# A transformer block in float32: fewer, larger transfers for each attention head, and softmax statistics through DRAM

## The chip, the cores and the metric

The kernel runs on one core of one Trainium2 chip. The metric is device microseconds of one execution; lower is better. A core has TensorE (PE, with its weight loads shown apart as PEld), VectorE (DVE), ScalarE (ACT), GpSimd (POOL) and SyncE (SP). SP does no arithmetic here: it issues nearly all DMA transfers, in the order of its own instruction stream, and sixteen DMA engines carry them out.

## The reference

One block of a model: normalization, one wide projection, a gated causal convolution of 31 taps, dilated attention of 16 heads, gates, an output projection, and a feed-forward part with a convolution of 3 taps. Sequence 1024, width 1024, head width 64, all in float32. What matters here is the attention:

```python
for window, dilation in ((128, 1), (512, 4), (2048, 16)):
    o_g, lse_g = dilated_window_attention(q, k, v, slopes, window, dilation)
    outs.append(o_g); lses.append(lse_g)
mix = jax.nn.softmax(jnp.stack(lses), axis=0)
o = jnp.einsum('gbsh,gbshd->bshd', mix, jnp.stack(outs))
y_b = o @ w_attn_out[l]
```

Each query sees keys at distances up to 128, every fourth up to 512, and every sixteenth up to 2048. Mixing three softmaxes by their log sums is the same as one softmax over all these keys, with a key counted once for each group that reaches it; the kernel computes that, with the counts and the distance slopes folded into a mask that is prepared on the host.

## The kernel before

Every float32 matrix product is made of rounded parts: an operand is split into a high part and a low part (`split`, L84), and the products high by high, high by low and low by high are summed. For the attention scores the two parts of the queries are interleaved on the 128 partitions (partition 2d holds the high part of channel d, 2d+1 the low part), so that one product with the high part of the keys, doubled onto both partitions, and one with the low part give the sum (`scored`, L922).

The stages, in order of time: normalization and the gated inputs; queries, keys and values (to about 410 us), whose parts go to DRAM scratch, `dq` and `dk` (L157, L158, written by `spill` in `qkv_tail`, L634) and `dv`; gates by a Strassen-like scheme while DVE runs the convolution; the attention (about 570 to 872 us); the output projections; the feed-forward part.

The attention loop (L1106 on) runs over slots `at`: 16 heads, two halves of the tokens, four steps each, so eight slots, called places 0 to 7, to a head. In places 0 to 3 the first 512 queries are scored against near keys. In place 4 come the far rows: for each of the four residues r modulo 4, queries of the second half against keys of the first half at multiples of 4 (`("far",)`). In places 5 to 7 the second half's near keys follow (blocks 7, 6, then 4 and 5). For each tile DVE adds the mask and takes the least value (`least`, L926), ACT makes the powers and their sum (`powers`, L964). The products with the values come twelve slots later (`BACK = 12`): the tiles are transposed on PE (`flip`, L1007), split by ACT and DVE into `ph` and `pl`, and multiplied by the values (`weigh`, L1041); `result` (L1057) copies the sum from PSUM and sends it to DRAM scratch `do_`. PE also has other work laid between by `fill`: gate and convolution-output products.

The second half of a head has near and far tiles with separate maxima and sums. Before the tiles are scaled, the two kinds must be brought together, and they lie in different orders: near statistics have one partition for each query of a block of 128, far statistics have one partition for each query of a residue class. `own` (L976) is a tile of 128 x 2 x 4 x 2 numbers: near or far, block or residue, least value or sum. `other` holds the counterparts in the other's order. `far_to_near` (L984) and `near_to_far` (L980) each move 4 KB in four transfers between them, `far_to_near` two slots after the far tile's slot, `near_to_far` one slot after the last near tile's. `compare` (L988) on DVE reads both nine slots after the far tile's slot, `combine` (L994) one slot later; then POOL scales the tiles (`times`, L967).

`head(h)` (L740) loads the next head's operands in place 1: for each part s of the queries, `q[s:P:2]`; for each partition parity s, the keys' high part to `kh[s:P:2]` and low part to `kl[s:P:2]`; and the mask. That is seven transfers. `values` (L905) loads the values in place 5 with two more. Each tile has two buffers. POOL makes reordered copies of a part of q, kh and kl for the far rows (`by_residue`, L918).

After the loop has issued its last scores, the outputs come back: `o_fetch` (L1073) loads the two parts of `do_` (products with the values' high and low part) for two channel blocks at a time, `o_step` (L1080) adds and splits them, and the product with the output weights `w_ao` follows. `w_ao` is laid out on the host (`_layout`).

Order: inside the attention loop ACT, DVE, PE and POOL follow the text (L1102). SP does not: its transfers are ordered by the framework's planner, which simulates the program and issues what is ready, earlier text first. A transfer that reads what another wrote, in DRAM too, waits on SP for that transfer to land.

Of the kernel before, what the change touches and what calls it, by code (L numbers as in the profile page):

```python
# [13 lines left out]
F32 = mybir.dt.float32  # L14
F32R = mybir.dt.float32r
# [6 lines left out]
P = 128  # L22
D = 1024
T = 1024
KT = D // P
H = 16
DH = 64
# [8 lines left out]
FRONT = (1, 1, 0, 0, 0, 0, 1, 0)  # L36
BEHIND = (1, 0, 1, 0, 2, 1, 1, 1)
BACK = 12
COPIES = (-1, 0, 1)
APART = (2, 3, 4, 5, 6)  # L40
START = (1, 1, 1, 1, 0, 0, 0, 0, 0, 0, 0, 0)
# [19 lines left out]
def block_kernel(ctx: ExitStack, tc: tile.TileContext, x, xT, x0, g2, pack, mask,  # L61
# [88 lines left out]
    def spill(dst, src):  # L150
        sp.dma_start(dst.bitcast(F32), src.bitcast(F32))

    def fetch(dst, src):
        sp.dma_start(dst.bitcast(F32), src.bitcast(F32))


    dq = [[dr.tile([P, 4, T], F32R, name=f"dq{i}_{a}") for a in range(2)] for i in range(2)]  # L157
    dk = [[dr.tile([P, 4, T], F32R, name=f"dk{i}_{a}") for a in range(2)] for i in range(2)]  # L158
    dv = [dr.tile([T, 8, P], F32R, name=f"dv{i}") for i in range(2)]
    dh = dr.tile([P, KT, T], F32, name="dh")  # L160
    db12 = [dr.tile([P, 4, 512], F32R, name=f"db12_{i}") for i in range(2)]
    dgate = [dr.tile([P, T], F32, name=f"dgate{i}") for i in range(16)]
    da = dr.tile([P, KT, T], F32, name="da")
    dya = [dr.tile([P, T], F32, name=f"dya{i}") for i in range(8)]
    do_ = [dr.tile([P, KT, T], F32, name=f"do{i}") for i in range(2)]
    dff = [dr.tile([P, T], F32, name=f"dff{i}") for i in range(FT)]
    dx2 = [dr.tile([P, D], F32, name=f"dx2_{i}") for i in range(8)]
    dform = [[dr.tile([P, 1024], F32R, name=f"dform{f}_{i}") for i in range(7)] for f in range(3)]

    HALVES = (slice(0, 512), slice(512, 1024))  # L170
# [134 lines left out]
    if True:  # L305
# [313 lines left out]
        def qkv_tail(ch, tt, qn):  # L619
            kind, g8 = ch % 3, ch // 3  # L620
            pt = big_ps(f"qt_{ch}_{tt}")[:, 0:512]
            for j in range(4):
                pe.transpose(pt[:, j * P : (j + 1) * P], qn[:, j * P : (j + 1) * P], ident)
            qh = p1a.tile([P, 512], F32R, tag="qh", bufs=2, name=f"qh_{ch}_{tt}")
            ql = p1a.tile([P, 512], F32R, tag="ql", bufs=2, name=f"ql_{ch}_{tt}")
            if kind == 0:
                act.activation(qh, pt, AF.Copy, scale=qkg)
                dve.scalar_tensor_tensor(out=ql, in0=pt, scalar=qkg, in1=qh.bitcast(F32),
                                         op0=ALU.mult, op1=ALU.subtract)
            else:  # L630
                split(qh, ql, pt)
            dst = dq if kind == 0 else dk
            for s, t in ((0, qh), (1, ql)):
                spill(dst[g8][s][:, :, tt * P : (tt + 1) * P], t.rearrange("p (a b) -> p a b", a=4))  # L634

        tails = []
        for ch in range(6):
# [102 lines left out]
        def head(h):  # L740
            hp, r, g8 = h // 2, (h % 2) * DH, h // 8
            q = p2.tile([P, T], F32R, tag="q", bufs=2, name=f"q_{h}")
            kh = p2.tile([P, T], F32R, tag="kh", bufs=2, name=f"kh_{h}")
            kl = p2.tile([P, T], F32R, tag="kl", bufs=2, name=f"kl_{h}")
            m = p2.tile([P, 640], F32, tag="m", bufs=2, name=f"m_{h}")
            for s in range(2):
                fetch(q[s:P:2, :], dq[g8][s][r : r + DH, hp % 4, :])
                fetch(kh[s:P:2, :], dk[g8][0][r : r + DH, hp % 4, :])
                fetch(kl[s:P:2, :], dk[g8][1][r : r + DH, hp % 4, :])
            sp.dma_start(m, mask[h])  # L750
            return q, kh, kl, m

        cover(COVER)
        firsts = [gate_weights(a)[1] for a, _ in PAIRS[:2]]
# [142 lines left out]
    if True:  # L897
# [82 lines left out]
        def near_to_far(h):  # L980
            for i in range(4):
                sp.dma_start(other[h][32 * i : 32 * i + 32, 1], own[h][:, 0, i])

        def far_to_near(h):  # L984
            for i in range(4):
                sp.dma_start(other[h][:, 0, i], own[h][32 * i : 32 * i + 32, 1])

        def compare(h):  # L988
            f = ready2("both", [P, 2, 4], F32, 2, f"both_{h}")
# [65 lines left out]
            return (h, half) if last else None  # L1055

        def result(h, half):  # L1057
            r = (h % 2) * DH
            o = outs.pop((h, half))
            cs = slice(half * 512, half * 512 + 512)  # L1060
            tmp = ready2("ot", [P, 512], F32, 2, f"ot_{h}_{half}")
            read_out[h, half] = act.activation(tmp.rearrange("p (i a r) -> p i a r", i=4, r=4),
                                               o.rearrange("p (i r a) -> p i a r", i=4, r=4), AF.Copy)
            for i in range(2):
                sp.dma_start(do_[i][r : r + DH, h // 2, cs], tmp[i * DH : (i + 1) * DH, :])

        def fill(n):
            for _ in range(n):
# [3 lines left out]

        def o_fetch(half, k):  # L1073
            cs = slice(half * 512, half * 512 + 512)
            raw = stage(do_[0][:, k : k + 2, cs], f"o_{half}{k}").rearrange("p (a b) -> p a b", a=2)
            hi, lo = (oT[i][half][:, k : k + 2, :] for i in range(2))
            fetch(lo, do_[1][:, k : k + 2, cs])
            return raw, hi, lo

        def o_step(new):  # L1080
# [21 lines left out]
        with tc.manual_schedule(engines={ENG.Activation, ENG.DVE, ENG.PE, ENG.Pool}):  # L1102
            apart = lambda at: at % 8 in APART or not 0 <= at < len(slots)
            pend = []
            fill(1)
            for at in range(len(slots) + BACK + 1):  # L1106
                count[2] += 1
                cur = slots[at] if at < len(slots) else None
                front, behind = (FRONT[at % 8], BEHIND[at % 8] + (START[at] if at < BACK else 0)) if cur else TAIL
                new = []  # L1110
                if cur is not None:
                    h, half, n = cur
                    place = at % 8
                    if place == 4:
                        statistics(h)
                    if place == 5:
                        values(h)
                    if place == 1 and h + 1 < H:
                        tiles[h + 1] = head(h + 1)
                    new = score(h, tiles[h], SCORES[half][n])  # L1120
                for unit in late:
                    share(*unit)
                if len(pieces) > 2 and apart(at):
                    piece_high(2)
                fill(front)
                for n, soon in enumerate(COPIES):
                    if at == 0 and soon < 0 or cur is not None and (at - soon) % 8 == 0 and at - soon < len(slots):
                        by_residue((at - soon) // 8 if at else 0, n)
                flips = []
                if BACK <= at < len(slots) + BACK:  # L1130
                    fh, fhalf, fn = slots[at - BACK]
                    if FLIPS[fhalf][fn]:
                        flips.append(flip(fh, fhalf, FLIPS[fhalf][fn]))
                for w in pend:
                    done = weigh(*w) or done
                pend = flips
                late = []
                if done is not None:
                    result(*done)
                    done = None  # L1140
                for ago, ready in ((BACK - 2, combine), (BACK - 3, compare)):
                    if 0 <= at - ago < len(slots) and slots[at - ago][1:] == (1, 0):
                        ready(slots[at - ago][0])
                for unit in new:
                    powers(*unit)
                if cur is not None and half == 0:
                    late = new
                for ago, n0, send in ((2, 0, far_to_near), (1, 3, near_to_far)):
                    if 0 <= at - ago < len(slots) and slots[at - ago][1:] == (1, n0):
                        send(slots[at - ago][0])  # L1150
                if at == len(slots):
                    p2_cm.__exit__(None, None, None)
                    hb2.append(ctx.enter_context(tc.tile_pool(name="hb2a", bufs=1, reuse_waits="tile")))
                    oT = [[hb2[0].tile([P, KT, 512], F32R, tag=f"hb{a}0", name=f"oT{a}0")] for a in range(2)]
                    heads = [o_fetch(0, k) for k in range(0, KT - 2, 2)]
                if at - len(slots) in (4, 5, 8, 9, 10, 11, 12):
                    o_step(heads)
                if at == len(slots) + BACK - 4:
                    heads.append(o_fetch(0, KT - 2))
                if apart(at):  # L1160
                    piece_low()
                fill(behind)
                if apart(at + 1):
                    piece_high(2)
            for _ in gates:
                piece_low()
                piece_high()
                o_step(heads)
# [579 lines left out]
def _layout(a):  # L1748
# [24 lines left out]
        "w_ch": w_ch,  # L1773
        "w_qkv": row(w_in[:, 2048:5120], 6),
        "w_co": col(a["w_conv_out"][0], 8),
        "w_ao": col(a["w_attn_out"][0], 8),
        "w_o": row(a["w_out"][0], 2),
        "w_up": col(a["w_up"][0], 2 * FT),
        "w_down": np.ascontiguousarray(a["w_down"][0].reshape(FT, P, D)),
# [13 lines left out]
```

## Time and profile before

| | |
|---|---|
| time, median of 3 runs | 1700.63 us (1699.92 to 1704.21) |
| profiled execution, its own time | 1702.94 us |
| its span, first to last instruction | 1701.1 us |
| mean granted TensorE clock | 0.998 |
| PE busy | 1685.4 us (99% of the span) |
| DVE, ACT, POOL busy | 1288.9, 786.0, 222.6 us |
| DMA: moved, mean rate | 300.21 MB, 176 GB/s |
| transfers of the statistics in all (`other<-own`) | 128, of 1 KB each |

The profile is one execution. A line of instructions gives its start, its duration, the engine, the line of the kernel, the operation with output and input tile, and, in square brackets, how long the engine had been idle before it and what ended that idle time. A line of waits gives the total in us, how many times, and the longest. On SP the duration of a transfer's line is that of the issue alone; the time from issue to landing is given apart.

### The profile page before, as it was taken

To read this page: it belongs to the slowest core of one execution; us is meant where nothing else is said; L and a number is where in the kernel's file an instruction comes from. 1 tells how busy PE (TensorE), PEld (TensorE's weight loads), DVE (VectorE), ACT (ScalarE), POOL (GpSimd) and SP (SyncE) were. 2 spreads that over 40 slices of the span, in tenths; PEclk is the share of its full clock that TensorE was granted. 3 is DMA by queue.
4 is the path that set the end of the run, shared out by engine and by line. 5 is a ranking of instruction groups with operands and counts; after the bars stand their busy time and mean duration, and the time that the engine had idled before them with its cause. 6 is when DMAs were issued, how large, how long until landed. Compare 5 with 4: busy or idle time off the path is not lost.

```text
span 1701.1 us, 22933 instructions
## 1 busy us (share of the span) xinstructions
PE 1685.4 (99%) x8003; PEld 1406.2 (83%) x8003; DVE 1288.9 (76%) x2098; ACT 786.0 (46%) x1351; POOL 222.6 (13%) x300
## 2 busy tenths in 40 slices
PE   9999999999999999999999999999999999999999
PEld 7888888888888888888878888888888888888887
DVE  5999999999876467756657654887777777889863
ACT  5411233233245477767745433554554455543431
POOL 0000132033000245445410000000000000000000
PEclk9999999999999999999999999999999999999999
DMA  9411145344555977777769694622222222498851
GB/s 373 152 50 50 50 136 161 124 136 137 186 170 196 312 218 240 246 226 232 209 191 340 202 337 143 235 87 87 75 87 87 86 76 80 153 382 302 289 167 50
DMA packets 186867, 300.21 MB, mean 176 GB/s; under 512 B 32000, under 2 KB 89984, under 8 KB 186240
## 3 DMA queue, kind: packets, MB, share of 16 engines
q1 hardware_dynamic: 185456, 294.43, 51.6%
q10 hardware_dynamic: 1296, 4.33, 0.6%
q8 instruction: 63, 1.03, 0.3%
q14 instruction: 52, 0.43, 0.1%
HBM read 214.67 MB, written 83.89 MB: 176 GB/s over the span
## 4 chain that ended last, share of the span: by engine, by line
PE 90%; DMA 5%; ACT 1%; DVE 1%; SPq 1%; issue 1%; POOL 0%; ACTq 0%; DVEq 0%; POOLq 0%
PE dx L1599 7%; PE xz L143 6%; PE xz L145 6%; PE xz L144 6%; PE dy L1599 5%; PE qkv L136 5%; PE qkv L138 5%; PE qkv L137 5%; PE y L145 2%; PE y L143 2%; PE y L144 2%; DMA kl<-dk 2%; PE wo L138 2%; PE wo L136 2%; PE wo L137 2%; PE pp L1014 1%
## 5 line engine op out<-in xcount | busy, mean ns | idle before, releaser
L136 PE MATMUL qkv<-hi_qkv,hT 128*128 128x512 f32 x384 | 151.2, 395 | 0.0
L138 PE MATMUL qkv<-hi_qkv,hT 128*128 128x512 f32 x384 | 149.8, 391 | 0.0
L137 PE MATMUL qkv<-lo_qkv,hT 128*128 128x512 f32 x384 | 149.8, 391 | 0.0
L1502 DVE SCALAR_TENSOR_TENSOR u<-u,pk 128x1023 f32<-128x1023 f32 x88 | 112.2, 1277 | 1.2 <-ACT u L1500 0.9
L112 POOL TENSOR_TENSOR rs<-ss,mhalf 128x8 f32<-128x8 f32 x32 | 66.2, 2072 | 294.3 <-DVE ss L111 294.3
L1036 DVE TENSOR_TENSOR pl<-pp,ph 128x512 fp32r<-128x512 f32 (+1 forms) x95 | 58.9, 620 | 47.4 <-ACT ph L1035 46.6
L585 DVE SCALAR_TENSOR_TENSOR cacc<-csum,both,cacc 128x512 f32<-128x512 f32 x120 | 89.3, 744 | 0.3
L585 DVE SCALAR_TENSOR_TENSOR cacc<-apad,pk,cacc 128x512 f32<-128x512 f32 x120 | 88.3, 744 | 0.0
L88 DVE TENSOR_TENSOR lo_uv<-raw_uv,hi_uv 128x1024 fp32r<-128x1024 f32 x20 | 24.5, 1226 | 79.5 <-ACT hi_uv L87 79.5
L138 PEld LDWEIGHTS qkv<-hi_qkv,hT 128*128 128x128 f32 x384 | 72.1, 188 | 15.0
L585 DVE SCALAR_TENSOR_TENSOR codd<-apad,pk,codd 128x513 f32<-128x513 f32 x112 | 83.6, 747 | 0.7 <-ACT codd L578 0.7
L137 PEld LDWEIGHTS qkv<-lo_qkv,hT 128*128 128x128 f32 x384 | 72.2, 188 | 14.3
L136 PEld LDWEIGHTS qkv<-hi_qkv,hT 128*128 128x128 f32 x384 | 72.1, 188 | 14.2
L1035 ACT ACTIVATE ph<-pp 128x512 fp32r<-128x512 f32 (+1 forms) x95 | 51.3, 540 | 45.4 <-PE pp L1014 45.2
L143 PE MATMUL xz<-h2left,hi_uv 128*128 128x512 f32 x176 | 68.6, 390 | 0.0
L143 PE MATMUL xz<-blk_t,hi_s3g 128*128 128x512 f32 x176 | 68.5, 389 | 0.0
L145 PE MATMUL xz<-h2left,lo_uv 128*128 128x512 f32 x176 | 68.5, 389 | 0.0
L144 PE MATMUL xz<-h2left,hi_uv 128*128 128x512 f32 x176 | 68.5, 389 | 0.0
L145 PE MATMUL xz<-blk_t,lo_s3g 128*128 128x512 f32 x176 | 68.5, 389 | 0.0
L144 PE MATMUL xz<-blk_t,hi_s3g 128*128 128x512 f32 x176 | 68.5, 389 | 0.0
L1500 ACT ACTIVATE u<-u,pk 128x1024 f32<-128x1024 f32 x44 | 54.5, 1238 | 9.5 <-DVE u L1489 4.5
L119 PE MATMUL ya<-aT,hi_co 128*128 128x512 f32 x128 | 53.6, 418 | 0.0
(486 smaller groups left out, 5076.8 us busy)
## 6 DMA issues: line engine op xcount, KB each, us to landing
wr<-w_down SPq DMA_DIRECT2D x45, 512.0 KB, 5.9
gr<-dff SPq DMA_DIRECT2D x62, 256.0 KB, 5.1
raw_qkv<-w_qkv SPq DMA_DIRECT2D x24, 512.0 KB, 5.2
dff<-u SPq DMA_DIRECT2D x22, 512.0 KB, 2.6
raw_uv<-w_up SPq DMA_DIRECT2D x21, 512.0 KB, 3.3
raw_ug<-w_up SPq DMA_DIRECT2D x20, 512.0 KB, 3.3
dv<-v SPq DMA_DIRECT2D x16, 512.0 KB, 2.9
q<-dq SPq DMA_DIRECT2D x32, 256.0 KB, 3.8
```

The costliest lines, as they stand in the source:

```text
L112: pool.tensor_tensor(out=dst, in0=tmp, in1=mhalf[:, : tmp.shape[1]], op=ALU.pow)
L136: pe.matmul(ps, ah, hi[:, k % 2, :], start=(k == 0), stop=False)
L137: pe.matmul(ps, ah, lo[:, k % 2, :], start=False, stop=False)
L138: pe.matmul(ps, al, hi[:, k % 2, :], start=False, stop=(k == KT - 1))
L143: pe.matmul(o, wh[:, k, :], bh[:, k, :], start=(start and k == 0), stop=False, skip_group_check=not start)
L144: pe.matmul(o, wh[:, k, :], bl[:, k, :], start=False, stop=False, skip_group_check=not start)
L145: end = pe.matmul(o, wl[:, k, :], bh[:, k, :], start=False, stop=(k == 3), skip_group_check=not start)
L585: dve.scalar_tensor_tensor(out=out_, in0=src[:, i : i + size], scalar=w(i), in1=out_, op0=ALU.mult, op1=ALU.add)
L1036: dve.tensor_tensor(out=runs(pl[:, c]), in0=order(pp[:, c]), in1=runs(ph[:, c]).bitcast(F32), op=ALU.subtract)
L1500: act.activation(acc, src, AF.Identity, bias=pk[:, C_FB + ci : C_FB + ci + 1], scale=w(2))
L1502: dve.scalar_tensor_tensor(out=acc[:, d:], in0=src[:, : T - d], scalar=w(2 - d), in1=acc[:, d:], op0=ALU.mult, op1=ALU.add)
L1599: pe.matmul(banks[n][:, cols], a[:, c], b[:, d], start=(start and i == 0 and m == 0), stop=(stop and i == nf - 1 and m == 2), skip_group_c ...
```

## The change

The high and low parts of queries and keys now lie in one scratch tensor each, with the part as an inner index, so that a partition order (channel, part) can be read as one run of rows. `head` loads q with one transfer of 128 partitions and the keys with two, each bringing high and low part into one tile `kk`. `result` sends both halves of its tile with one transfer: the scratch tensor `do_` is stored as channel block, part, row, token, with the two heads of a block interleaved by row; the rows of `w_ao` are reordered on the host to match. The far rows' statistics no longer go from SBUF to SBUF in four transfers: `far_out` writes them to a small DRAM tensor `dstat` with one transfer, where `far_to_near` stood, and `far_to_near` reads them back in the near order with one transfer, written five slots after the far tile's slot (`READ = 5`). `near_to_far` is as before.

```diff
+READ = 5
-    dq = [[dr.tile([P, 4, T], F32R, name=f"dq{i}_{a}") for a in range(2)] for i in range(2)]
-    dk = [[dr.tile([P, 4, T], F32R, name=f"dk{i}_{a}") for a in range(2)] for i in range(2)]
+    dq, dk = ([dr.tile([P, 2, 4, T], F32R, name=f"{n}{i}") for i in range(2)] for n in ("dq", "dk"))
-    do_ = [dr.tile([P, KT, T], F32, name=f"do{i}") for i in range(2)]
+    do_ = dr.tile([KT, 2, P, T], F32, name="do")
+    dstat = [dr.tile([P, 4, 2], F32, name=f"dstat{i}") for i in range(2)]
...
-                spill(dst[g8][s][:, :, tt * P : (tt + 1) * P], t.rearrange("p (a b) -> p a b", a=4))
+                spill(dst[g8][:, s, :, tt * P : (tt + 1) * P], t.rearrange("p (a b) -> p a b", a=4))
...
-            kh = p2.tile([P, T], F32R, tag="kh", bufs=2, name=f"kh_{h}")
-            kl = p2.tile([P, T], F32R, tag="kl", bufs=2, name=f"kl_{h}")
+            kk = p2.tile([P, 2, T], F32R, tag="kk", bufs=2, name=f"kk_{h}")
             m = p2.tile([P, 640], F32, tag="m", bufs=2, name=f"m_{h}")
+            fetch(q, dq[g8].rearrange("p s c t -> (p s) c t")[2 * r : 2 * r + P, hp % 4, :])
             for s in range(2):
-                fetch(q[s:P:2, :], dq[g8][s][r : r + DH, hp % 4, :])
-                fetch(kh[s:P:2, :], dk[g8][0][r : r + DH, hp % 4, :])
-                fetch(kl[s:P:2, :], dk[g8][1][r : r + DH, hp % 4, :])
+                fetch(kk[s:P:2], dk[g8][r : r + DH, :, hp % 4, :])
             sp.dma_start(m, mask[h])
-            return q, kh, kl, m
+            return q, kk[:, 0], kk[:, 1], m
...
+        def far_out(h):
+            sp.dma_start(dstat[h % 2], own[h][:, 1])
+
         def far_to_near(h):
-            for i in range(4):
-                sp.dma_start(other[h][:, 0, i], own[h][32 * i : 32 * i + 32, 1])
+            sp.dma_start(other[h][:, 0], dstat[h % 2].rearrange("(i a) r s -> (a r) i s", i=4))
...
-            for i in range(2):
-                sp.dma_start(do_[i][r : r + DH, h // 2, cs], tmp[i * DH : (i + 1) * DH, :])
+            sp.dma_start(do_[h // 2].rearrange("i (d r) t -> (i d) r t", r=2)[:, h % 2, cs], tmp)
...
-            raw = stage(do_[0][:, k : k + 2, cs], f"o_{half}{k}").rearrange("p (a b) -> p a b", a=2)
+            part = lambda i: do_[k : k + 2, i, :, cs].rearrange("k p t -> p k t")
+            raw = stage(part(0), f"o_{half}{k}").rearrange("p (a b) -> p a b", a=2)
...
-                for ago, n0, send in ((2, 0, far_to_near), (1, 3, near_to_far)):
+                for ago, n0, send in ((2, 0, far_out), (1, 3, near_to_far), (READ, 0, far_to_near)):
...
-        "w_ao": col(a["w_attn_out"][0], 8),
+        "w_ao": col(a["w_attn_out"][0].reshape(KT, 2, DH, D).swapaxes(1, 2).reshape(D, D), 8),
```

More of the change, by code (lines that the diff above doesn't have):

```diff
@@ L1057, in result @@
         def result(h, half):
-            r = (h % 2) * DH
             o = outs.pop((h, half))
@@ L1074, in o_fetch @@
             cs = slice(half * 512, half * 512 + 512)
-            raw = stage(do_[0][:, k : k + 2, cs], f"o_{half}{k}").rearrange("p (a b) -> p a b", a=2)
+            part = lambda i: do_[k : k + 2, i, :, cs].rearrange("k p t -> p k t")
+            raw = stage(part(0), f"o_{half}{k}").rearrange("p (a b) -> p a b", a=2)
             hi, lo = (oT[i][half][:, k : k + 2, :] for i in range(2))
-            fetch(lo, do_[1][:, k : k + 2, cs])
+            fetch(lo, part(1))
             return raw, hi, lo
```

## The prediction

> **What bounds the kernel now.** I read the page first, then the stretch of the trace in which the changed lines run (attention, 600 to 872 us), then who waits there, then SP's queue.
>
> ```profile
> span 1701.1 us, 22933 instructions
> PE 1685.4 (99%) x8003; PEld 1406.2 (83%) x8003; DVE 1288.9 (76%) x2098; ACT 786.0 (46%) x1351; POOL 222.6 (13%) x300
> PE 90%; DMA 5%; ACT 1%; DVE 1%; SPq 1%; issue 1%; POOL 0%; ACTq 0%; DVEq 0%; POOLq 0%
> ```
>
> TensorE is the bound, with 15.7 us of idle in the whole span; no change to transfers alone can win more than that and what a lower clock costs. The changed lines act in the attention stage. The table of stretches (span, then busy time of PE, PEld, DVE, ACT, POOL, then granted clock, DMA share, GB/s) and PE's waits between 560 and 920 us:
>
> ```profile
> 600.00:872.00 272.00, 265.77 (x1607) 230.93 (x1606) 172.24 (x625) 193.22 (x560) 128.88 (x221) 0.99 0.74 224
> ...
> 729.00:738.00 9.00, 6.82 (x21) 5.15 (x20) 2.68 (x10) 3.13 (x9) 5.81 (x11) 0.62 0.85 262
> ```
>
> ```profile
> PE s L924 <- DMA kl<-dk: 3.5, 6, 1.0
> PE o L1053 <- DVE pl L1036: 2.9, 6, 1.1
> PE s L923 <- issue: 1.2, 1, 1.2
> PE yb L119 <- DVE gg L1209: 0.8, 1, 0.8
> PE s_far L924 <- POOL fars L920: 0.7, 1, 0.7
> ```
>
> PE idles 272.00 - 265.77 = 6.2 us in the stage, mostly because the first score of a head (L923, L924) waits for that head's keys: six heads, 3.5 us, and once 1.2 us more. In one head the wait also lowers the clock: 0.62 over 9 us.
>
> Why are the keys late? Each head's transfers are issued by SP alone, in order. The queue around that worst head, with the events it serves:
>
> ```profile
> 705.84 0.39 ACT L965 ACTIVATE pf<-pf,own 128x128 f32<-128x128 f32 x1
> ```
>
> ```profile
> 712.88 0.61 SPq L986 DMA_DIRECT2D other<-own  x1
> ...
> 720.09 0.54 SPq L154 DMA_DIRECT2D q<-dq  x1
> ...
> 721.36 1.19 SPq L1065 DMA_DIRECT2D do<-ot  x2
> 722.64 1.31 SPq L982 DMA_DIRECT2D other<-own  x2
> 724.04 0.55 SPq L154 DMA_DIRECT2D kl<-dk  x1
> 724.65 0.59 SPq L154 DMA_DIRECT2D q<-dq  x1
> 725.29 0.59 SPq L154 DMA_DIRECT2D kh<-dk  x1
> 725.92 0.59 SPq L154 DMA_DIRECT2D kl<-dk  x1
> 726.56 0.58 SPq L750 DMA_DIRECT2D m<-mask  x1
> ```
>
> ```profile
> 711.41 0.40 PE L923 MATMUL s<-kh,q 128*128 128x512 f32 x1
> ...
> 727.94 0.39 PE L1053 MATMUL o<-pl,v 128*128 128x256 f32 x1 [0.57 <-DVE pl L1036]
> ...
> 730.39 0.47 PE L923 MATMUL s<-kh,q 128*128 128x512 f32 x1 [1.16 <-issue]
> 731.89 0.77 PE L924 MATMUL s<-kl,q 128*128 128x512 f32 x1 [1.02 <-DMA kl<-dk]
> 732.45 0.63 PE L119 MATMUL ya<-aT,hi_co 128*128 128x512 f32 x1
> 732.88 0.63 PE L120 MATMUL ya<-aT,hi_co 128*128 128x512 f32 x1
> ```
>
> SP issues back to back, one per 0.635 us (724.65, 725.29, 725.92). The far statistics, final at about 706.4 (705.84 plus the last read of an accumulator), leave at 712.88: SP is 6.5 us behind. The last piece of keys leaves at 725.92 and is used 6.0 us later, at 731.89. So in this stage it is the number of issues on SP that decides when keys arrive, not their bytes.
>
> ```profile
> v<-dv SPq DMA_DIRECT2D x14, 512.0 KB, 7.2
> do<-ot SPq DMA_DIRECT2D x56, 128.0 KB, 4.0
> kl<-dk SPq DMA_DIRECT2D x27, 256.0 KB, 4.7
> q<-dq SPq DMA_DIRECT2D x26, 256.0 KB, 3.6
> m<-mask SPq DMA_DIRECT2D x14, 320.0 KB, 5.7
> other<-own SPq DMA_DIRECT2D x120, 1.0 KB, 3.4
> ```
>
> These are the stage's transfers with their median time to landing. 120 of them move one kilobyte each.
>
> **The change part by part.** A head issues today 6 + 1 (queries, keys, mask), 2 (values), 4 (outputs) and 8 (statistics), 21 in all, plus some 2.4 of the work laid between. After: 3 + 1, 2, 2 and 4 + 1 + 1, 14 in all. Seven issues fewer at 0.635 us is 4.4 us of SP's time in a head that takes 19.0 us here (711.41 to 730.39) and 17.2 without PE's waits of 0.57 and 1.16; the queue's need falls from (21 + 2.4) x 0.635 = 14.9 us, beside waits of its own, to 10.4 us.
>
> Loads of q and keys: same bytes, same 4 KB rows, twice the size per transfer. A 512 KB load may land later than a 256 KB one: between q's 3.6 us and the 7.2 of v. I take 5.7, the mask's, which is nearest in bytes per row. That is 1.0 us later than kl's 4.7, but the last key load now leaves at least 4.4 us earlier, and the lag of 6.5 us should run off over the first heads. The keys' wait needs 2.2 us at most (1.16 + 1.02). All six waits go: **-3.5 and -1.2 us**. What is late next is PE itself: the next wait in the list is DVE's pl.
>
> Clock: in 729 to 738 PE worked 6.82 us at 0.62, worth 6.82 x 0.38 = 2.6 us; the matmuls of 512 columns follow one another at 0.43 us there (732.45, 732.88). With no idle before it the drop goes: **-2.6 us**. The Trainium skill (TensorE: Matmul & The Clock Gate, Part 1) says that the gate judges activity in a free-running window, so that the same kernel meets it or not from one execution to the next. The trace shows one drop in six such waits, which agrees; by that rule a median run may not have had it, and its sum would lack this term.
>
> Outputs: one issue of 256 KB for two of 128 KB. At the end of the stage the chain runs through them:
>
> ```profile
> 880.08 1.22 DVE L1090 TENSOR_TENSOR raw_o<-raw_o,oT 128x1024 f32<-128x1024 f32 x1 [1.03 <-DMA oT<-do]
> ```
>
> ```profile
> 881.83 0.45 PE L1053 MATMUL o<-pl,v 128*128 128x384 f32 x1 [1.13 <-DVE pl L1036]
> ```
>
> DVE waits 1.03 us for the reload of the outputs and PE then 1.13 us for DVE. One issue less brings that reload 0.6 us forward at best, or not at all if the larger write lands later; I take half, **-0.3 us**, and the same for the wait of 0.8 us at the first yb behind it: **-0.3 us**. The new layout of the outputs and the reordered weight rows cost nothing on the chip: same row lengths of 2 KB, and the weights are reordered on the host. The spills of q and k keep their number and size; they run under the projections, far from any wait.
>
> Statistics: near to far is unchanged. Far to near becomes a write of 4 KB to DRAM (L986's place) and, three slots later in the text, one gather of 512 pieces of 8 bytes. Two issues for four, but a new wait: SP must see the write landed before it issues the read, and all of SP's queue stands behind it (near rows' statistics, next queries and keys, outputs). The nearest rows:
>
> ```profile
> DMA to landing us min/median/max: 1.8/4.4/7.3
> ```
>
> That is L986, the transfer that it replaces. If the planner puts the read directly behind the write, SP stands for 4.4 us less what lies between (one issue, 0.6): 3.8 us. The queue then needs 10.4 + 3.8 = 14.2 us of 17.2, still under today's 14.9; cost on PE nothing. In the worst row, 7.3 us, it is 17.1, which just fills the head. The cover is the 17.2 us that PE needs for a head; while the queue needs less, nothing shows on PE, and each microsecond above it costs PE one. SP does not follow the text: it takes what is ready.
>
> ```profile
> L92 SPq DMA_DIRECT2D raw_o<-do x3: 554/619/631, 780.9 to 816.7; - x3
> ```
>
> These loads are written at the end of the loop, near 860 us, and issue from 780.9. So I expect the read soon after the write, well ahead of its user, `compare`. Two legs of 4.4 us from 706.4 end at 715.8; `compare` wants them at 724.6:
>
> ```profile
> 725.98 0.17 DVE L990 TENSOR_TENSOR both<-own,other 128x8 f32<-128x8 f32 x1 [1.36 <-DMA other<-own]
> ```
>
> Here it already waited 1.36 us for near statistics issued at 722.64, and PE's 0.57 at 727.94 follows from it. With SP up to date that goes: **-0.6 us**. The Trainium skill (DMA: Bandwidth & Descriptors, Anatomy of one DMA) speaks against the detour: completion of a write to HBM can be surprisingly long. The rows give 4.4 us for the same bytes under load; the sum by the page's fixed part of about 2 us would be no other.
>
> At the first head the stage opens with SP late and PE once waits 0.7 us for POOL's fars behind it; the detour adds a leg there. Between -0.7 (wait gone) and +3.8 (a whole added leg shown), I take **+0.5**, since SP has fewer issues just there too.
>
> Sum: -3.5 - 1.2 - 2.6 - 0.3 - 0.3 - 0.6 + 0.5 = -8.0 us. The profiled execution took 1702.94 us (span 1701.1 and 1.8 around it), so 1694.9. It is 2.3 us above the median of 1700.63; if the profiler makes that difference, the median goes to 1692.6, if the clock drop does, to 1695. I predict **1694.0**.
>
> **The rivals.** First, the stalls are mostly the profiled execution's own, or the loads stay late because the DMA engines are the limit (share 0.74 in the stage, 0.85 in the worst head). For it: the 2.3 us above the median, about the clock's 2.6. Against: SP's lag is in every head shown. The gain over the median is then 8.0 - 2.6 - half of 4.7, about 3: 1697.5.
>
> Second, slower: far statistics arrive after `compare`. If the read is issued where it is written, behind the next queries, keys and mask, and SP still lags, it leaves 4.4 us (seven issues) before today's end of the mask's issue (726.56 + 0.58), at 722.7, and lands 4.4 us later at 727.1: 2.5 us after 724.6. PE paid 0.57 for 1.36 us of lateness, so at least 1.05 us a head; 15 heads, 16 us; with the rest of the gains, 1702.9 - 8.0 + 16 = 1711. It decides where the read is issued later than 8.8 us after the head's first score (13.2 from 711.41 to 724.6, less 4.4). Against it: the readiness order of SP, and that the lag itself goes.
>
> Third, the reordered queue shifts what the planner places outside the hand-ordered loop: no row prices it; I let it widen the range by 2 us.
>
> **How the numbers follow.** Forecast 0.60 (1689 to 1695.5, mean of both bases), first rival 0.22 (1695.5 to 1701), slower rival 0.18. 0.3% is 5.1 us, about what a measurement can tell from no change: faster below 1695.5, slower above 1705.7. The range 1687 to 1705 leaves out the slower rival and little else. Faster 0.58, same 0.24, slower 0.18.
>
> **What would show it.** In the profile after: about 14 issues a head from the changed lines; key loads landing well ahead of the first score and no PE wait on the key tile; PE idle in the stage near 2 us and clock 1.00 throughout; SP waiting for the write of the statistics, by some microseconds a head, and nobody behind it. Wrong if DVE waits at L990 in most heads (slower rival), if SP's wait exceeds 7 us a head, or if the key waits persist with SP idle (then the DMA engines were the limit).

## The result, and the profile after

| | before | after |
|---|---|---|
| median | 1701.38 us (12 runs, 1699.25 to 1704.92) | 1705.41 us (12 runs, 1702.66 to 1707.51) |
| profiled execution, its own time | 1702.94 us | 1704.01 us |
| its span | 1701.1 us | 1702.2 us |

The ratio is 1.0019, with a 95% interval from 1.0011 to 1.0028: slower, by less than the 0.3% that was set as the bound of "same", and 11 us above the forecast. The range of the prediction ended at 1705.0.

The page of the changed kernel answers to the three lines shown of before:

```profile
span 1702.2 us, 22749 instructions
PE 1684.6 (99%) x8003; PEld 1406.7 (83%) x8003; DVE 1289.3 (76%) x2098; ACT 786.5 (46%) x1351; POOL 221.5 (13%) x300
PE 92%; DMA 4%; DVE 1%; ACT 1%; issue 1%; POOL 0%; SPq 0%; ACTq 0%; DVEq 0%
```

PE's idle in the span is now 17.6 us (1702.2 - 1684.6); it was 15.7. The table of stretches (busy time of PE, PEld, DVE, ACT, POOL, granted clock, DMA share, GB/s) puts the loss into the attention stage, where PE idles 9.5 us (272.00 - 262.46) and idled 6.2; one stretch again has a lower clock:

```profile
600.00:872.00 272.00, 262.46 (x1594) 228.59 (x1593) 169.90 (x618) 192.86 (x556) 128.39 (x219) 0.99 0.75 224
```

```profile
720.00:740.00 20.00, 18.08 (x104) 15.69 (x102) 12.26 (x42) 12.96 (x38) 9.66 (x16) 0.91 0.69 202
```

PE's waits in the whole span (total, times, longest):

```profile
PE o L1054 <- DVE pl L1037: 7.3, 9, 1.9
PE s L922 <- DMA kk<-dk: 2.7, 2, 1.5
...
PE yb L120 <- DVE gg L1209: 0.9, 1, 0.9
PE s_far L923 <- POOL fars L919: 0.7, 1, 0.7
```

The waits for keys fell, from 3.5 and 1.2 us to 2.7 and 0.2. In their place PE waits for `pl`, DVE's part of the transposed tiles: 7.3 us where it was 2.9. Two more lists say why: what DVE waited for at the comparison, and what SP waited for, both between 600 and 872 us:

```profile
DVE both L991 <- DMA other<-own: 9.1, 4, 2.7
...
DVE both L991 <- DMA kk<-dk: 5.0, 3, 2.6
...
DVE both L991 <- DMA dgate<-gs: 1.5, 1, 1.5
```

```profile
SPq L987 <- DMA dstat<-own: 71.8, 15, 5.9
```

The comparison waited in 8 of 16 heads, 15.6 us together; before, it waited once, 1.4 us. The list puts a wait down to the transfer that landed last before it. The comparison reads neither keys nor gates: in all eight heads it began within 0.2 us of the landing of the last near statistics, and the far ones had landed at least 6.2 us earlier.

SP stands before the read of the statistics in every head, 4.8 us each (71.8 / 15), until the write has landed. This is SP's queue in the head whose first score is at 713.92; a line is the issue alone:

```profile
713.19 0.45 SPq L984 DMA_DIRECT2D dstat<-own  x1
713.73 0.41 SPq L249 DMA_DIRECT2D dya<-ya  x1
720.12 0.37 SPq L987 DMA_DIRECT2D other<-dstat  x1
720.59 1.26 SPq L981 DMA_DIRECT2D other<-own  x2
721.95 0.53 SPq L155 DMA_DIRECT2D q<-dq  x1
722.57 0.55 SPq L155 DMA_DIRECT2D kk<-dk  x1
723.22 0.54 SPq L1064 DMA_DIRECT2D do<-ot  x1
723.81 1.53 SPq L981 DMA_DIRECT2D other<-own  x2
```

From 714.1 to 720.1 it issues nothing. Behind the read stand the near rows' statistics (L981), the last two of them issued from 723.81. The comparison on DVE needs them, and PE needs what DVE does next:

```profile
729.94 0.17 DVE L991 TENSOR_TENSOR both<-own,other 128x8 f32<-128x8 f32 x1 [2.71 <-DMA other<-own]
```

```profile
731.91 0.53 PE L1054 MATMUL o<-pl,v 128*128 128x256 f32 x1 [1.92 <-DVE pl L1037]
```

DVE was ready at 727.23 (729.94 - 2.71) and waited 2.71 us; PE lost 1.92 of them. The last near statistics were issued at 724.45 and took 5.4 us to land, behind the merged loads and outputs; in the head shown of before the last ones took 2.5 us (723.34 to 725.80).

### The profile page after: what moved, and what is told of

It reads as the page before. It is cut to its first block, busy times and chain, and to the rows that moved or that the text cites. A ratio compares the mean times of both kernels' runs of the same rounds, so it can differ in the third digit from the quotient of the medians.

```text
span 1702.2 us, 22749 instructions
## 1 busy us (share of the span) xinstructions
PE 1684.6 (99%) x8003; PEld 1406.7 (83%) x8003; DVE 1289.3 (76%) x2098; ACT 786.5 (46%) x1351; POOL 221.5 (13%) x300
## 4 chain that ended last, share of the span: by engine, by line
PE 92%; DMA 4%; DVE 1%; ACT 1%; issue 1%; POOL 0%; SPq 0%; ACTq 0%; DVEq 0%
PE dx L1599 7%; PE xz L145 6%; PE xz L144 6%; PE xz L146 6%; PE dy L1599 5%; PE qkv L137 5%; PE qkv L139 5%; PE qkv L138 5%; PE y L145 2%; PE y L144 2%; PE y L146 2%; PE wo L138 2%; PE wo L139 2%; PE wo L137 2%; PE pp L1015 2%; PE gx L144 1%
## 5 line engine op out<-in xcount | busy, mean ns | idle before, releaser
L138 PEld LDWEIGHTS qkv<-lo_qkv,hT 128*128 128x128 f32 x384 | 72.2, 188 | 14.2
```

The source lines that it names most:

```text
L138: pe.matmul(ps, ah, lo[:, k % 2, :], start=False, stop=False)
```

## The experiments

Two theories were to be told apart. **The hold**: SP stands in order before the read of the statistics, and what it holds up (near statistics, keys) comes late; fewer issues by themselves are a gain. **Larger transfers**: merged transfers land later (in the profile after, outputs of 256 KB took a median of 6.9 us to land where those of 128 KB took 4.0, keys 6.1 where they took 4.7), and that is the cost. All ratios are to the kernel before on the same chip, with 95% intervals.

**Far statistics direct, loads and outputs merged.** The changed kernel, with the four transfers of before put back:

```diff
-        def far_out(h):
-            sp.dma_start(dstat[h % 2], own[h][:, 1])
         def far_to_near(h):
-            sp.dma_start(other[h][:, 0], dstat[h % 2].rearrange("(i a) r s -> (a r) i s", i=4))
+            for i in range(4):
+                sp.dma_start(other[h][:, 0, i], own[h][32 * i : 32 * i + 32, 1])
...
-                for ago, n0, send in ((2, 0, far_out), (1, 3, near_to_far), (READ, 0, far_to_near)):
+                for ago, n0, send in ((2, 0, far_to_near), (1, 3, near_to_far)):
```

> The changed kernel with the far rows' statistics sent as before (four transfers from SBUF to SBUF), loads and outputs merged. Theory (SP is held in front of the DRAM read: 71.8 us over 15 heads in the changed kernel, and the near statistics queued behind it reach the comparison late): the hold is gone and SP still issues 5 fewer a head than before; compare waits and PE's waits for pl fall to about those of the kernel before (3 us) or below, the key waits stay under 2 us; 1696 us, ratio to before 0.997. Rival (the larger transfers land later, outputs 6.8 us against 4.0, and that is what costs): the loss of 3 us stays, about 1704 us, ratio 1.002.

Measured: 1690.74 us, ratio 0.9934 [0.9919, 0.9948]. The stage has hardly a stall left; stretches and PE's waits of this version:

```profile
600.00:860.00 260.00, 259.03 (x1597) 227.80 (x1596) 171.24 (x620) 191.99 (x557) 127.80 (x219) 1.00 0.78 234
```

```profile
PE o L1050 <- DVE pl L1033: 1.7, 4, 0.9
PE early L465 <- POOL ones L344: 1.0, 1, 1.0
PE s_far L921 <- POOL fars L917: 0.7, 1, 0.7
```

No wait for keys, none at the comparison, none at yb (the product with the output weights), clock 1.00. Yet the transfers land about as late as in the changed kernel, outputs after 6.0 us (6.9 there) and keys after 6.4 (6.1 there):

```profile
kk<-dk SPq DMA_DIRECT2D x26, 512.0 KB, 6.4
do<-ot SPq DMA_DIRECT2D x29, 256.0 KB, 6.0
```

So later landing costs nothing where SP is not held, and the whole loss, and more than the whole, comes with the detour through DRAM. Whether the later landing of the near statistics adds to the price of the hold in the changed kernel was not separated. That the gain is larger than either theory expected also says that the kernel before lost more to SP than its waits for keys.

**The detour alone.** The kernel before with `far_out`, `far_to_near` and `READ` of the change, nothing else of it.

> The kernel before with the statistics through DRAM alone; loads and outputs in small transfers as before. Theory (the hold): SP needs (19 + 2.4) x 0.635 = 13.6 us of issues and about 4.8 us of hold in a head of 17.2 us, so it becomes the bound of the stage by about 1.2 us a head and more where it waits for other things; 1715 us, between 1708 and 1730, ratio 1.008; DVE waits at the comparison in most heads. Rival (larger transfers are what costs): two issues fewer, nothing larger, about 1700 us, ratio 0.999.

Measured: 1725.80 us, ratio 1.0142 [1.0124, 1.0161]: the slowest of all, although it issues two transfers fewer a head than before. The hold is enough by itself, with small transfers. PE waits for the keys' second and first part, and SP for the write:

```profile
PE s L926 <- DMA kl<-dk: 12.5, 10, 2.2
...
PE s L925 <- DMA kh<-dk: 3.3, 3, 1.5
```

```profile
SPq L990 <- DMA dstat<-own: 60.8, 14, 5.6
```

The comparison waited in 6 heads only, not in most as was expected; DVE waited more for masks, 20.0 us in 7 waits.

**The read behind the near statistics.** The changed kernel; only the read's place in SP's queue is tied down:

```diff
+        near_sent = {}
         def near_to_far(h):
-            for i in range(4):
-                sp.dma_start(other[h][32 * i : 32 * i + 32, 1], own[h][:, 0, i])
+            near_sent[h] = [sp.dma_start(other[h][32 * i : 32 * i + 32, 1], own[h][:, 0, i]) for i in range(4)]
...
-            sp.dma_start(other[h][:, 0], dstat[h % 2].rearrange("(i a) r s -> (a r) i s", i=4))
+            with ExitStack() as behind:
+                for sent in near_sent.pop(h):
+                    behind.enter_context(tc.issue_after(sent.ins))
+                sp.dma_start(other[h][:, 0], dstat[h % 2].rearrange("(i a) r s -> (a r) i s", i=4))
```

> The changed kernel with the read of the statistics queued behind the last of the near statistics (the planner then puts it behind the next mask), so SP has the write landed when it comes to it. Theory (the hold): SP's wait for the write falls from 71.8 us to under 10, the near statistics are on time; if the read itself still lands before the comparison, 1695 us, ratio 0.996; if it is now the last to land, DVE waits for it in part of the heads and the gain is smaller, 1700. Rival (larger transfers): 1704 us, ratio 1.002.

Measured: 1690.53 us, ratio 0.9932 [0.9919, 0.9945]. Same transfers, same sizes, same number of issues as the changed kernel, 15 us less. SP no longer waits for the write; the read, which landed after a median of 6.1 us here, is now the last to reach the comparison, but costs DVE only this much, and PE nothing that shows:

```profile
DVE both L995 <- DMA other<-dstat: 0.7, 2, 0.5
```

**The loads alone, the outputs alone.** The kernel before with only q and the keys merged, and with only the outputs merged (the lines of the diff that concern them).

> The kernel before with q in one and the keys in two transfers alone; outputs and statistics as before. Theory (the hold is the cost, fewer issues are the gain): three issues fewer a head, 1.9 us; the waits for keys mostly gone, 1697 us, ratio 0.9975. Rival (larger transfers land later): key loads late, 1701 to 1704 us, ratio 1.000 to 1.002.

> The kernel before with the outputs of a half head in one transfer alone; loads and statistics as before. The loads alone gave 0.9945 with three issues fewer a head, loads and outputs together 0.9934 with five. If only the number of SP's issues counts, two fewer are worth 1.3 us of SP's time a head and much of the same stalls go: 1695 us, ratio 0.996. If the loads count for themselves (they are what is late), the outputs give little: 1700 us, ratio 0.999. If the larger output transfers cost something that the loads' gain covers, above 1.000.

Measured: loads 1692.55 us, 0.9945 [0.9931, 0.9959]; outputs 1690.45 us, 0.9935 [0.9922, 0.9948]. Either one gives what both give. The outputs are not what PE waits for, and still their merging takes all waits for keys away: what they share with the keys is SP's queue.

**Issues put back.** The version with merged outputs, and behind each output transfer one or two transfers of 1 KB that nobody needs (`range(1)`, and `range(2)` in the other version):

```diff
+            for i in range(1):
+                extra = p2b.tile([32, 8], F32, tag="extra", bufs=8, name=f"extra_{h}_{half}_{i}")
+                sp.dma_start(extra, tmp[32 * i : 32 * i + 32, 0:8])
```

> The version with merged outputs alone (0.9935 of before), with one added transfer of 1 KB from the output tile to a tile that nobody reads, behind each output transfer: the number of SP's issues is that of the kernel before again, the large output transfers stay. If the number of issues is what put the kernel before over the edge: about 1701 us, ratio 1.000. If the output transfers' own landing or size made the gain: 1691 us, ratio 0.994.

> The same with two added transfers behind each output transfer, two issues a head more than the kernel before. If SP's queue is the bound there: 2 x 0.635 us in each of 15 heads, 19 us, less what little slack is left: 1715 to 1722 us, ratio 1.008 to 1.012, with most heads waiting for keys. If issues cost nothing by themselves: 1691 us, ratio 0.994.

Measured: with two issues more a head 1699.31 us, 0.9985 [0.9976, 0.9994]; with four more 1720.59 us, 1.0108 [1.0094, 1.0122]. With four, PE's waits for keys are back, larger than in the kernel before:

```profile
PE s L924 <- DMA kl<-dk: 9.5, 8, 1.8
PE o L1053 <- DVE pl L1036: 5.9, 8, 2.0
PE s L923 <- DMA kh<-dk: 3.6, 3, 2.5
```

From 21 to 23 issues a head the time rises by 21 us, where two issues of 0.635 us in 15 heads are 19. That the two are so near is partly luck. From the second head's first score to the last head's (two issues put back, then four):

```profile
592.30:832.70 240.40, 236.09 (x1439) 205.87 (x1437) 158.82 (x591) 179.24 (x525) 120.91 (x204) 0.99 0.78 233
```

```profile
592.30:855.10 262.80, 244.55 (x1438) 210.04 (x1437) 158.47 (x591) 178.83 (x523) 120.64 (x203) 0.97 0.70 212
```

PE idles 13.9 us more (18.2 against 4.3), and the same matmuls take 8.5 us longer, at a granted clock of 0.97 against 0.99. Below 19 issues nothing more is to be had.

**The hold alone.** Far statistics direct, loads and outputs merged, and beside them the write to DRAM and a read into a tile that nobody uses; then the same with the read tied behind the near statistics as above.

```diff
+        def far_out(h):
+            sp.dma_start(dstat[h % 2], own[h][:, 1])
+        def read_back(h):
+            unused[h] = p2b.tile([P, 4, 2], F32, tag="unused", bufs=2, name=f"unused_{h}")
+            sp.dma_start(unused[h], dstat[h % 2].rearrange("(i a) r s -> (a r) i s", i=4))
...
+                for ago, n0, send in ((2, 0, far_to_near), (2, 0, far_out), (1, 3, near_to_far), (READ, 0, read_back)):
```

> Loads and outputs merged and the far statistics sent directly (the version that took 0.9934 of before), with the write of the far statistics to DRAM and the read back added beside it; the read goes to a tile that nobody uses, so nobody waits for its data. Only SP's wait in front of the read and two more issues are left of the detour. If the hold of SP is the cost: SP waits some 4 to 5 us a head again, the near statistics and keys behind it are late, and the time goes to the changed kernel's or above, 1705 to 1712 us, ratio 1.002 to 1.006. If the late far statistics themselves were the cost: two issues more, 1692 us, ratio 0.994.

> The version with the unused write and read beside direct far statistics (0.9984 of before), with the read queued behind the last of the near statistics, as in the pinned version. The same transfers, the same number of issues, only the place of the read in SP's queue differs. If the 8 us above the version without the detour are SP standing in front of the read: 1691 us, ratio 0.993. If they are the two issues more: 1699 us, ratio 0.998.

Measured: 1699.17 us, 0.9984 [0.9973, 0.9995], and with the read tied behind 1690.68 us, 0.9936 [0.9923, 0.9950]. The two hold the same transfers, and nobody waits for what is read. The 8.5 us between them are the price of the read's place in the queue. The first is less than was expected: four other issues now stand between the far statistics' end and the write, and the write lands sooner, so that SP stands less:

```profile
SPq L992 <- DMA dstat<-own: 9.6, 7, 1.6
```

The write's landing in this version (L988):

```profile
DMA to landing us min/median/max: 1.7/3.5/4.5
```

**The place in the text.** The changed kernel with `READ = 8`.

> The changed kernel with READ = 8 for 5: in the text the read of the statistics stands three slots later, behind the next head's loads and one slot ahead of the comparison. If the place in the text decides when SP comes to it, the hold is gone as in the pinned version, 1691 us, ratio 0.993. If the planner brings the read forward to where the write is done in its own simulation, SP's queue is as in the changed kernel and so is the time: 1705 us, ratio 1.002, with some 70 us of SP waiting for the write.

Measured: 1705.93 us, 1.0023 [1.0014, 1.0033], the changed kernel's time, with the same wait of SP:

```profile
SPq L987 <- DMA dstat<-own: 72.0, 15, 5.8
```

The three slots in the text change nothing. That the planner brings the read forward to where the write is done in its own simulation was the expectation, and fits; the simulation itself is not shown.

All versions together, with the issues a head of the lines concerned (before: 21):

| version | issues | SP waits for the write | ratio |
|---|---|---|---|
| pinned read | 14 | no | 0.9932 |
| far direct, loads and outputs merged | 16 | none | 0.9934 |
| the same, with unused write and read tied behind | 18 | no | 0.9936 |
| loads alone | 18 | none | 0.9945 |
| outputs alone | 19 | none | 0.9935 |
| the unused write and read, read brought forward | 18 | yes, shorter | 0.9984 |
| outputs alone, two issues put back | 21 | none | 0.9985 |
| before | 21 | none | 1 |
| the change | 14 | 4.8 us a head | 1.0019 |
| the change, READ = 8 | 14 | 4.8 us a head | 1.0023 |
| outputs alone, four issues put back | 23 | none | 1.0108 |
| detour alone | 19 | 4.3 us a head | 1.0142 |

The pinned version and the one with direct far statistics beat both kernels, by 0.7% against before, and the outputs alone do so as well.

## Why the prediction was wrong, point by point

**SP's queue bounds the stage: right.** The prediction read it from the spacing of the issues and the lag. The outputs alone, and the issues put back, show it. So does the lag: the far statistics left 6.5 us after they were final in the head shown of before, still 6.0 us in the changed kernel's (final at 707.22, sent at 713.19), and at most 0.7 us in the version with direct far statistics.

**The gain of fewer issues: right in kind, too small.** The sum had -8.0 us for everything. Without the detour's hold it is 0.66%, 11 us (8.9 to 13.8 by the interval). All six waits for keys, the drop of the clock and the wait at yb went, as the terms said. Two terms were too small. From the second head's first score to the last head's, before and with direct far statistics:

```profile
593.10:837.00 243.90, 237.44 (x1439) 206.85 (x1437) 159.22 (x591) 178.91 (x523) 119.94 (x203) 0.99 0.75 230
```

```profile
592.50:826.90 234.40, 232.79 (x1439) 205.16 (x1438) 159.13 (x591) 178.51 (x523) 119.72 (x203) 1.00 0.82 245
```

The same work takes 9.5 us less: PE idles 4.9 us less (6.5 against 1.6) and is busy 4.6 us less. The clock was at 0.50 for 6.8 us, in which PE was busy for 6.01; that is 3.0 us, where the sum had 2.6 from the mean over 9 us. The remaining 1.6 us of busy time had no term. At the reload of the outputs and the first yb, between the matmuls at 877.3 and at 912.9 us of before, the same matmuls take 1.8 us less with direct far statistics, where the sum had 0.6.

**The hold: the step that failed.** "The queue then needs 10.4 + 3.8 = 14.2 us of 17.2 [...]; cost on PE nothing." Three things were wrong with it. First the size: the landing was taken from the old transfers of the statistics, 4.4 us; the write took 5.8:

```profile
DMA to landing us min/median/max: 4.6/5.8/6.9
```

With the measured hold of 4.8 us the same sum is 10.4 + 4.8 = 15.2 us, above the 14.9 of the kernel before: the change gave SP nothing back. The Trainium skill (DMA: Bandwidth & Descriptors, Anatomy of one DMA) warns, in a section on transfers that GpSimd issues, that completion of a write to HBM can be surprisingly long. The runs do not show that the target made this write slow: with the unused read the same write landed after a median of 3.5 us, and after 1.7 where it was fastest. What goes with it is what SP had issued before and was still in flight: 768 to 2368 KB in the changed kernel, 259 to 1284 KB there.

Second the cover. The prediction says "while the queue needs less, nothing shows on PE", with the 17.2 us of a head as the cover. By the same sum the outputs alone need 13.6 us and lose nothing that shows, the kernel before needs 14.9 and loses 11 us against them, and with four issues put back the need is 16.1 and the loss about 30 us. PE is held up well below 17.2; SP also waits for other things, in order, which the sum leaves out. The prediction had read a lag of 6.5 us at 14.9 and still took 17.2 as the cover.

Third, and worse, the sum over a head treats SP's time as one pool. What stands behind the read has a due time inside the head: the near statistics had 727.23 to land by, went out from 723.81 and landed at 729.86. A wait placed ahead of them costs even where the head's total would fit: the unused read behind the near statistics cost nothing, ahead of them 8.5 us. The prediction named what is queued behind the wait, and then did not give each of them its own due time.

**The far statistics in time: right.** The read landed 1.9 us after its issue, at 722.0 in the head shown, against 727.23. That it would issue soon after the write was foretold too; it was counted as good, and is what does the harm.

**The rival that ended slower: right engine, wrong transfer.** It had the statistics arrive after the comparison because the far ones are read late, at 1711 us. It was the near ones, because the far ones are read early. Its price of 16 us on top of the gains is near the 14.7 us between the changed kernel and the one with direct far statistics (1705.41 - 1690.74); that is luck, since it counted 15 late comparisons for another reason, and 8 were late.

**The rival of slow large transfers: refuted as a cause by itself.** Merged loads and outputs land later, as was allowed for (5.7 us taken, 6.1 measured for the keys), and in the versions with merged loads and no hold PE never waits for keys.

**Smaller terms.** The wait for POOL's fars at the first head stayed at 0.7 us in every version, so the term of +0.5 was 0. The wait at the first yb stayed at 0.9 with the change; it was 1.4 with the loads alone and gone with the outputs alone. The drop of the clock came back (0.91 over 20 us), right behind the 1.92 us for which PE idled until 731.91: 0.50 for 3.4 us from 732.0.

## What to carry to other kernels

Count the issues on the queue that feeds a stage and set them against the stage's period, with the queue's own waits: here, near the edge, two issues more a head cost 0.5% (19 to 21) and 1.2% (21 to 23), and below the edge nothing was left to win. A transfer that must wait for another holds everything behind it in that queue, so place it behind whatever is due sooner, and check each of those against its own due time, not against the sum. Where a planner orders the queue, the place in the text does not; tie the order down.

## What the runs showed of the hardware that was not expected

Issuing a transfer cost SP about 0.635 us back to back, from 1 KB to 512 KB alike. 19 issues of the lines concerned and some 2.4 others a head (13.6 us) did not hold PE up, 21 (14.9 us) did, in a head that takes 16.7 us when nothing waits (234.40 us for 14 heads with direct far statistics). The Trainium skill (DMA: Bandwidth & Descriptors, Issuing engines are not separate DMA queues) calls the time to initiate a transfer usually small beside the transfer itself. Beside landings of 1.9 to 7.5 us (medians) it is small here too; but the issues follow one another on SP while the landings overlap, and so they helped to bound the stage.

In every trace of this case at most eight of SP's transfers were in flight. In the kernel before, between 600 and 837 us, SP waited 21 times, 13.2 us, for a transfer to land, and each time it was the one issued eight before. So a transfer that lands late can hold SP too, whatever its use; whether the chip or the program sets the eight, and how much of the stage's limit it makes, no run shows.

A write of 4 KB to DRAM needed 4.6 to 6.9 us to land in the changed kernel and 1.7 to 4.5 us in the version with the unused read, where less was in flight ahead of it. Its read back, 512 pieces of 8 bytes, landed after 1.9 us where SP had stood idle before it, and after a median of 6.1 us in the pinned version, where it went out behind the next loads.
